# A fused encoder layer on one core: where writes are queued, how weights are cut, and who searches for used tiles

## Chip, cores and metric

One core of one Trainium2 chip runs the kernel as a single program. The metric is the device time of one execution in microseconds, the median of several runs. Each run of the profiler shows one execution.

## The reference

One layer on 256 tokens of width 2048, in fp32. First a residual block: RMSNorm, a projection, trailing mean pools on one half of the columns and eight-head latent attention with a block-causal mask on the other, and an output projection. Then the part around which this change turns, a retrieval over 128 x 128 single-neuron experts:

```python
q = (xn @ w_pq).reshape(B, S, PEER_HEADS, 2, PEER_HALF)
s1 = einsum('bshd,hnd->bshn', q[..., 0, :], sub_k1)
s2 = einsum('bshd,hnd->bshn', q[..., 1, :], sub_k2)
v1, i1 = top_k(s1, 16); v2, i2 = top_k(s2, 16)
vs, ci = top_k((v1[..., :, None] + v2[..., None, :]).reshape(B, S, 8, 256), 16)
eidx = e1 * 128 + e2            # per token: 8 heads x 16 experts
gates = softmax(vs)
act = gelu(einsum('tkd,td->tk', expert_u[eidx], xn))
y = einsum('tk,tkd->td', act * gates, expert_v[eidx])
```

Last, a gate on the layer's own input p: `h + sigmoid(RMSNorm(h) @ w_ple_gate) * (p @ w_ple_proj)`.

## The kernel before, in words

**Products.** TensorE (PE) computes every large product in fp32 accuracy from three passes over split operands: `hi` is the value rounded to fp32r (ScalarE, ACT, L101) and `lo` the rest (VectorE, DVE, L103; now and then GpSimd, POOL). Weights come as units of 128 x 2048 fp32 (1 MB), each used in two parts of 1024 columns. The class `Feed` (L61 to L112) does the loading, two units ahead of the one in use, into three buffers `raw`, all on the queue of SyncE (SP) except the very first unit; it splits two parts ahead into three buffers each of `hi` and `lo`. `mm3` (L213) issues the three matmuls.

**Experts.** The kernel computes the hidden value of all tokens for 112 of the 128 expert tiles densely (the loop at L1441, `feat_mm`, 48 matmuls of 256 columns a tile), and for the last 16 tiles (`NP`, `P0` = 104) only for the pairs that were chosen. Beside the dense tiles run two lists of tasks: `side` (one task per `hook`, two to four hooks a tile) and `lq` for the chosen pairs (0.65 of a task per hook, `PAIR_PACE`).

- *One-hot groups* (`group_hots` L986, `group` L1001): for each of 64 groups of four tokens DVE compares indices with column numbers (two operations at L993) and multiplies by two bf16 parts of the gate (two at L996), ACT makes the third part (L227); 12 bf16 matmuls (L1006) turn them into the gates of all 128 tiles, which DVE multiplies into the activations (L1012) and ACT copies elsewhere (L1014, L1017). Every second group the gates of the 16 pair tiles are written to the tensor `gateD` (L1019).
- *Pairs* (`pair_loads` L1079, `pair_step` L1094): 9 chunks of 128 rows, 8 steps each. POOL gathers a half row of xn per row (`xr`, one buffer) for every four steps and a half row of U (`ur`, two buffers) for every step, two steps ahead; DVE takes the dot product (L1097). After a chunk POOL scatters its four columns of sums to `hidD` (L1104). At the end four quarters are read back, passed through gelu, multiplied by the gates and written to the coefficient tensor `coefD` (L1107 to L1136).
- *Used search and lists*: when the groups are through (about tile 67), `used` (L1189) looks in blocks of eight tiles for pairs of expert and token block with any coefficient; `classes` to `indices` (L1218 to L1337) build lists of the rows of V that are needed, in three stages (tiles 0 to 79, 80 to 119, 120 to 127).
- *Values*: 97 list tiles of V (`v_tile` L1407); POOL gathers rows of V (L1363) and coefficients (L1376). Eleven of them run between the last dense tiles. Half of the V rows use the `raw` buffers of `Feed`.

**Order.** SP's queue keeps the order in which the program emits it; the other engines are ordered by the framework's scheduler, except in two stretches written by hand. Every DMA waits on its issuing queue until its data and its buffer are ready, and what is queued behind it on that engine waits as well. The writes to `coefD` of the dense tiles (L1170) stay on SP's queue in both versions.

Of the kernel before, what the change touches and what calls it, by code (L numbers as in the profile page):

```python
# [8 lines left out]
F32 = mybir.dt.float32  # L9
# [10 lines left out]
P = 128  # L20
# [40 lines left out]
class Feed:  # L61


    def __init__(self, nc, pool, units, loads=2, splits=2, on_pool=()):
        self.nc, self.pool, self.units = nc, pool, units
        self.loads, self.splits, self.on_pool = loads, splits, on_pool
        self.raw = {}
        self.parts = [(u, i) for u, (_, cols, parts, _) in enumerate(units) for i in range(parts)]
        self.ready = deque()
        self.n_load = self.n_split = self.n_got = 0  # L70
        self.end = len(units)

    def load(self, upto):
        while self.n_load < min(upto + 1, self.end):
            src, cols, parts, by_part = self.units[self.n_load]
            if callable(src):
                self.raw[self.n_load] = src()
                self.n_load += 1
                continue
            raw = self.pool.tile([P, 2048], F32, name="raw", tag="raw")  # L80
            w = cols // parts
            if by_part:
                for i in range(parts):
                    self.nc.scalar.dma_start(raw[:, i * w:(i + 1) * w], src[:, i * w:(i + 1) * w])
            else:
                self.nc.sync.dma_start(raw[:, :cols], src)
            self.raw[self.n_load] = raw
            self.n_load += 1

    def split(self, upto):  # L90
        while self.n_split < min(upto + 1, len(self.parts)):
            u, i = self.parts[self.n_split]
            if u >= self.end:
                break
            self.load(u)
            _, cols, parts, _ = self.units[u]
            w = cols // parts
            r = self.raw[u][:, i * w:(i + 1) * w]
# [8 lines left out]
    def get(self):  # L107
        u, _ = self.parts[self.n_got]
        self.load(u + self.loads)
# [5 lines left out]
def emit(tc, a):  # L115
# [82 lines left out]
    feed_v = Feed(nc, strm, [(lambda c=c, i=i: vst["load"](c, i), D, 2, False) for c, i in order[BETWEEN:]], loads=3,  # L198
# [99 lines left out]
    feed.load(0)  # L298
# [377 lines left out]
    e1T = gt.tile([P, T, 2], BF16, name="e1T")  # L676
    e2T = gt.tile([P, T, 2], BF16, name="e2T")
    gT = gt.tile([P, 2, T, 2], BF16, name="gT")
# [4 lines left out]
    iotab = gt.tile([P, P], BF16, name="iotab")  # L683
# [3 lines left out]
    iota1 = gt.tile([P, P], BF16, name="iota1")  # L687
    for lo, hi, base in ((0, P0, 0), (P0, ND, STAGES[2]), (ND, NE, P0)):
        pool.iota(iota1[:, lo:hi], pattern=[[1, hi - lo]], base=base, channel_multiplier=0,
# [149 lines left out]
    def pair_chunks():  # L839
# [5 lines left out]
        for t in range(2):  # L845
            sp.dma_start(listD[t * P * NCH:(t + 1) * P * NCH, :].rearrange("(p k) c -> p (k c)", k=NCH), kd[:, t, :])
# [61 lines left out]
    def slots_T(t):  # L908
# [4 lines left out]
        dve.tensor_copy(e1T[:, ts, :], pt[:, 0:P, None].to_broadcast([P, P, 2]))  # L913
        dve.tensor_copy(e2T[:, ts, :], pt[:, P:2 * P, None].to_broadcast([P, P, 2]))
# [4 lines left out]
        for i in range(3):  # L919
            dve.tensor_copy(part, rest)  # L920
            if i < 2:
                dve.tensor_copy(gT[:, i, ts, :], part[:, :, None].to_broadcast([P, P, 2]))
# [63 lines left out]
    def group_hots(g):  # L986
        wk = st["wk"]
        sh = [P, 4, 64, 2]
        tk = slice(4 * g, 4 * g + 4)
# [11 lines left out]
    def group(g):  # L1001
# [16 lines left out]
        if g % 2 == 1:  # L1018
            sp.dma_start(gateD[:, g // 2].rearrange("p n t -> p (n t)"), st["gs"].rearrange("p n t -> p (n t)"))  # L1019
# [5 lines left out]
    lst = {"n": 0, "x": {}, "u": {}}  # L1025
    steps = [(s, half, i) for s in range(NS) for half in range(2) for i in range(4)]

    def pairs_index():
        lp = st["lp"]
        zt = lp.tile([P, ring_w], F32, name="xr", tag="xr")[:, :1024]  # L1030
        pool.memset(zt, 0.0)
        for i in range(0, NP * T, 1024):
            sp.dma_start(hid_pairs[:, i:i + 1024], zt[:, :min(1024, NP * T - i)])
# [9 lines left out]
    def pairs_index2():  # L1043
        lp, keys = st["lp"], lst["keys"]
        n = 4 * NS
        scr = lp.tile([P, ring_w], F32, name="xr", tag="xr")
# [32 lines left out]
    def pair_loads(k):  # L1079
# [4 lines left out]
        if i == 0:  # L1084
            x = lp.tile([P, ring_w], F32, name="xr", tag="xr")[:, :1024]
# [8 lines left out]
    def pair_step(k):  # L1094
# [5 lines left out]
        if half == 1 and i == 3:  # L1100
            hp = lst["hp"][:, :, s]
            dve.tensor_tensor(hp[:, 0], hp[:, 0], hp[:, 1], op=OP.add)
            for c in range(4):
                pool.indirect_dma_start(out=hidD, out_offset=bass.IndirectOffsetOnAxis(  # L1104
                    ap=lst["hidx"][:, s, c:c + 1], axis=0), in_=hp[:, 0, c:c + 1], in_offset=None)

    def pair_load_coefs(q):  # L1107
        lp = st["lp"]
# [3 lines left out]
        sp.dma_start(hq, hid_pairs[:, q * w:(q + 1) * w])  # L1112
        sp.dma_start(gq, gateD.rearrange("p a n t -> p (a n t)")[:, q * w:(q + 1) * w])
        lst["hg"] = hq, gq

    def pair_coefs(q):
# [4 lines left out]
        cq = lp.tile([P, ring_w], F32, name="xr", tag="xr")[:, :NP * 64].rearrange("p (n t) -> p n t", t=64)  # L1121
# [6 lines left out]
        sp.dma_start(coef_rows[1][:, P0 - N0:P0 - N0 + NP, 64 * q:64 * q + 64], cq)  # L1128
# [60 lines left out]
    def used(lo, hi, b):  # L1189
# [3 lines left out]
        tc.keep_in_program_order(dve.tensor_reduce(  # L1193
# [614 lines left out]
```

## Time and profile before

| | |
|---|---|
| median of 3 runs | 1670.56 us (1669.11 to 1674.48) |
| the profiled execution | 1667.58 us, of which the span from first to last instruction is 1665.8 us |
| mean granted clock of TensorE | 0.978 |
| busy: PE, DVE, ACT, POOL | 1580.7, 1253.8, 884.8, 448.6 us |
| moved by DMA | 396.20 MB, mean 238 GB/s |

The span falls into stages: the attention block up to about 230 us, the search for experts to 383, the dense expert tiles to about 1215 (those with groups and most pair steps from 552 to 898), the values to about 1560, the gate to the end. A busy engine says little here: what a stage costs is read from the idle time of PE, from who ended it, and from the granted clock.

### The profile page before, as it was taken

The page shows a single profiled execution, that of the slowest core. Times are in us where ns is not written, and L with a number is a line of the kernel's source. Part 1 is how long each engine was busy: PE and PEld are TensorE (multiplying, and loading weights), DVE is VectorE, ACT ScalarE, POOL GpSimd, SP SyncE. Part 2 cuts the span into 40 slices and gives each one's busy share as a digit, 9 for nine tenths or more (in the row PEclk, how much of TensorE's full clock was granted, in tenths as well). Part 3 has the DMA queues.
Part 4 walks back from the last instruction along what each step waited for, and adds up shares of the span by engine and source line. Part 5 has one row for each costly group of instructions (what it writes and reads, how often), then busy time and mean ns, then how long its engine had stood idle before and what let it go on. Part 6 is the DMA issues. An engine that isn't in the chain of part 4 may idle for free.

```text
span 1665.8 us, 27633 instructions
## 1 busy us (share of the span) xinstructions
PE 1580.7 (95%) x10548; PEld 1426.5 (86%) x10548; DVE 1253.8 (75%) x2360; ACT 884.8 (53%) x1615; POOL 448.6 (27%) x372
## 2 busy tenths in 40 slices
PE   8999999999999998978888989999989999999998
PEld 6888788999999997867788989999868888888886
DVE  6575667999997887867788868867787667667764
ACT  7765445544544665645454333445455565566653
POOL 0010000000000334533334320032247676676000
PEclk9999999999999999979989999999999999999999
DMA  8652356555555686857668987878679888888462
GB/s 302 222 199 102 127 214 241 178 171 184 178 181 182 214 272 235 261 194 257 231 227 317 351 326 240 291 293 284 206 269 338 288 294 298 282 298 288 152 225 105
DMA packets 82160, 396.20 MB, mean 238 GB/s; under 512 B 19523, under 2 KB 24772, under 8 KB 43620
## 3 DMA queue, kind: packets, MB, share of 16 engines
q1 hardware_dynamic: 48148, 233.87, 39.6%
q0 software_dynamic: 32000, 157.48, 27.5%
q10 hardware_dynamic: 1872, 3.02, 0.5%
q8 instruction: 84, 1.38, 0.3%
q14 instruction: 56, 0.46, 0.1%
HBM read 367.01 MB, written 27.32 MB: 237 GB/s over the span
## 4 chain that ended last, share of the span: by engine, by line
PE 72%; DMA 12%; DVE 8%; issue 3%; ACT 3%; POOL 1%; SPq 0%; DVEq 0%; ACTq 0%; POOLq 0%
PE bank L216 23%; PE bank L215 23%; PE bank L214 23%; DMA raw<-in_U 5%; DMA ur<-in_UP,uidx 3%; DVE lo L103 3%; DVE ur L1097 2%; ACT hi L101 2%; DMA xr<-xnD,rowx 2%; DMA raw<-in_w_in_q 1%; DVE oo L996 1%; PE bank L1310 1%; DVE oo L993 1%; PE bank L1006 1%; DMA raw<-in_w_out 1%
## 5 line engine op out<-in xcount | busy, mean ns | idle before, releaser
L101 ACT CAST hi<-raw 128x1024 fp32r<-128x1024 f32 (+2 forms) x466 | 479.0, 1032 | 460.2 <-PE bank L215 261.8
L103 DVE TENSOR_TENSOR lo<-raw,hi 128x1024 fp32r<-128x1024 f32 (+2 forms) x466 | 558.0, 1201 | 197.2 <-ACT hi L101 195.8
L214 PE MATMUL bank<-xnH,hi 128*128 128x256 f32 x1792 | 522.2, 292 | 6.0 <-ACT hi L101 6.0
L216 PE MATMUL bank<-xnH,lo 128*128 128x256 f32 x1792 | 518.2, 290 | 6.6 <-DVE lo L103 6.4
L215 PE MATMUL bank<-xnL,hi 128*128 128x256 f32 x1792 | 516.2, 288 | 0.0
L214 PEld LDWEIGHTS bank<-xnH,hi 128*128 128x128 f32 x1792 | 351.2, 196 | 8.5 <-ACT hi L101 6.9
L216 PEld LDWEIGHTS bank<-xnH,lo 128*128 128x128 f32 x1792 | 350.3, 196 | 9.5 <-DVE lo L103 8.8
L215 PEld LDWEIGHTS bank<-xnL,hi 128*128 128x128 f32 x1792 | 351.2, 196 | 0.3
L215 PE MATMUL bank<-lo,ccH 128*128 128x512 f32 x520 | 206.3, 397 | 1.1 <-DVE lo L103 1.1
L216 PE MATMUL bank<-hi,ccL 128*128 128x512 f32 x520 | 205.7, 396 | 0.0
L103 DVE TENSOR_TENSOR lo<-vraw,hi 128x1024 fp32r<-128x1024 f32 x108 | 131.4, 1224 | 51.0 <-ACT hi L101 49.7
L1376 POOL DMA_INDIRECT cr<-coefD,idx x97 | 127.5, 1315 | 144.4 <-DVE idx L1337 73.0
L214 PE MATMUL bank<-hi,ccH 128*128 128x512 f32 x520 | 154.5, 395 | 1.1 <-ACT hi L101 1.1
L101 ACT CAST hi<-vraw 128x1024 fp32r<-128x1024 f32 x110 | 115.1, 1049 | 64.6 <-PE bank L216 41.6
L1090 POOL DMA_INDIRECT ur<-in_UP,uidx x72 | 85.2, 1184 | 168.9 <-DVE hp L1097 134.3
L1097 DVE CUSTOM_DVE_ANT_0 ur<-ur,xr 128x1024 f32<-128x1024 f32 x72 | 87.6, 1220 | 56.7 <-DMA xr<-xnD,rowx 28.6
L215 PEld LDWEIGHTS bank<-lo,ccH 128*128 128x128 f32 x520 | 98.3, 189 | 24.7 <-DVE lo L103 2.3
L214 PEld LDWEIGHTS bank<-hi,ccH 128*128 128x128 f32 x520 | 97.5, 189 | 24.0 <-ACT hi L101 2.0
L216 PEld LDWEIGHTS bank<-hi,ccL 128*128 128x128 f32 x520 | 98.3, 189 | 22.3
L1006 PE MATMUL bank<-oo 128*128 128x128 bf16 x768 | 75.7, 228 | 39.7 <-DVE oo L996 37.5
L227 ACT ACTIVATE oo<-oo,gT 128x128 bf16<-128x128 bf16 x256 | 82.4, 399 | 46.7 <-DVE oo L996 45.9
L1006 PEld LDWEIGHTS <-oo 128*128 128x128 bf16 x768 | 49.1, 101 | 50.9 <-DVE oo L996 37.1
(398 smaller groups left out, 2474.6 us busy)
## 6 DMA issues: line engine op xcount, KB each, us to landing
raw<-in_U SPq DMA_DIRECT2D x112, 1024.0 KB, 5.6
raw<-in_w_out SPq DMA_DIRECT2D x16, 1024.0 KB, 4.9
raw<-in_w_pq SPq DMA_DIRECT2D x16, 1024.0 KB, 4.9
raw<-in_w_gate SPq DMA_DIRECT2D x16, 1024.0 KB, 5.0
raw<-in_w_in_p SPq DMA_DIRECT2D x8, 1024.0 KB, 4.8
coefD<-CA SPq DMA_DIRECT2D x8, 1024.0 KB, 12.0
coefD<-CB SPq DMA_DIRECT2D x5, 1024.0 KB, 10.6
raw<-in_w_in_kv SPq DMA_DIRECT2D x8, 576.0 KB, 4.6
```

Source lines behind the costliest of these rows:

```text
L101: self.nc.scalar.copy(hi[:, :w], r)
L103: eng.tensor_tensor(lo[:, :w], r, hi[:, :w].bitcast(F32), op=OP.subtract)
L214: pe.matmul(ps, ah, bh, start=start, stop=False)
L215: pe.matmul(ps, ah, bl, start=False, stop=False)
L216: pe.matmul(ps, al, bh, start=False, stop=stop)
L227: act.activation(dst, ps, AF.Copy, scale=scale)
L993: dve.tensor_tensor(pairs(dst), cols.rearrange("p (i c) -> p i c", c=2)[:, None].to_broadcast(sh), e[:, tk, None, :].to_broadcast(sh), op= ...
L996: dve.tensor_tensor(pairs(oo[:, k]), pairs(m1), gT[:, k, tk, None, :].to_broadcast(sh), op=OP.mult)
L1006: pe.matmul(pt[:, i * P:(i + 1) * P], o2, o1[k], start=(k == 0), stop=(k == 2))
L1090: pool.indirect_dma_start(out=u, out_offset=None, in_=a["UP"], in_offset=bass.IndirectOffsetOnAxis(ap=lst["uidx"][:, half, s, i:i + 1], ax ...
L1097: dve.tensor_tensor_reduce(out=u, in0=u, in1=lst["x"][s, half], scale=1.0, scalar=0.0, op0=OP.mult, op1=OP.add, accum_out=lst["hp"][:, hal ...
L1376: pool.indirect_dma_start(out=cr[:, :w], out_offset=None, in_=src, in_offset=bass.IndirectOffsetOnAxis(ap=row(c, i, 1), axis=0))
```

## The change

Seven edits in one diff, all of them shown in their core:

- `Feed` loads parts (half units) instead of units: five buffers of 1024 columns instead of three of 2048, five parts ahead.
- V rows that used the `raw` buffers get three buffers `vraw2` of their own, in the space of the last stage.
- Writes (and the reads of the pair quarters) move from SP's queue: `gateD` to ACT's, `xnD`, `listD`, the zeros of `hidD`, the pair quarters and their coefficients to POOL's; the last are written in two halves.
- `xr` gets two buffers.
- The scatters to `hidD` are queued and issued one at a time at odd steps; what is left goes before the quarters are read.
- The two index tables and the two gate tables each become one, so that two wide operations make the one-hots of a group.
- `used` becomes eight ACTIVATEs with accumulation on ACT, except for the last stage.

```diff
 class Feed:
...
+    def __init__(self, nc, pool, units, loads=5, splits=2, on_pool=()):
...
     def load(self, upto):
-        while self.n_load < min(upto + 1, self.end):
-            src, cols, parts, by_part = self.units[self.n_load]
+
+        while self.n_load < min(upto + 1, len(self.parts)):
+            u, i = self.parts[self.n_load]
+            if u >= self.end:
+                break
+            src, cols, parts, by_part = self.units[u]
+            w = cols // parts
+            cs = slice(i * w, (i + 1) * w)
             if callable(src):
...
-            raw = self.pool.tile([P, 2048], F32, name="raw", tag="raw")
...
+                raw = self.pool.tile([P, 1024], F32, name="raw", tag="raw", bufs=5)[:, :w]
+                (self.nc.scalar if by_part else self.nc.sync).dma_start(raw, src[:, cs])
             self.raw[self.n_load] = raw
             self.n_load += 1
...
     def get(self):
-        u, _ = self.parts[self.n_got]
-        self.load(u + self.loads)
+        self.load(self.n_got + self.loads)
         self.split(self.n_got + self.splits)
...
-        sp.dma_start(xnD[t * P:(t + 1) * P, :], h[t])
+        pool.dma_start(xnD[t * P:(t + 1) * P, :], h[t])
...
     def group_hots(g):
...
-        for dst, cols, e in ((m1, iota1, e1T), (oo[:, 3], iotab, e2T)):
-            dve.tensor_tensor(pairs(dst), cols.rearrange("p (i c) -> p i c", c=2)[:, None].to_broadcast(sh),
-                              e[:, tk, None, :].to_broadcast(sh), op=OP.is_equal)
-        for k in range(2):
-            dve.tensor_tensor(pairs(oo[:, k]), pairs(m1), gT[:, k, tk, None, :].to_broadcast(sh), op=OP.mult)
+        sh = [P, 2, 4, 64, 2]
+
+        def pairs2(x):
+            return x.rearrange("p a t (i c) -> p a t i c", c=2)
+
+        dve.tensor_tensor(pairs2(oo[:, 2:4]), iotas.rearrange("p a (i c) -> p a i c", c=2)[:, :, None].to_broadcast(sh),
+                          eT[:, g][:, :, :, None, :].to_broadcast(sh), op=OP.is_equal)
+        dve.tensor_tensor(pairs2(oo[:, 0:2]), pairs(m1)[:, None].to_broadcast(sh),
+                          gT[:, g][:, :, :, None, :].to_broadcast(sh), op=OP.mult)
...
-            sp.dma_start(gateD[:, g // 2].rearrange("p n t -> p (n t)"), st["gs"].rearrange("p n t -> p (n t)"))
+            act.dma_start(gateD[:, g // 2].rearrange("p n t -> p (n t)"), st["gs"].rearrange("p n t -> p (n t)"))
...
-            x = lp.tile([P, ring_w], F32, name="xr", tag="xr")[:, :1024]
+            x = lp.tile([P, ring_w], F32, name="xr", tag="xr", bufs=2)[:, :1024]
...
-            for c in range(4):
-                pool.indirect_dma_start(out=hidD, out_offset=bass.IndirectOffsetOnAxis(
-                    ap=lst["hidx"][:, s, c:c + 1], axis=0), in_=hp[:, 0, c:c + 1], in_offset=None)
+            lst["out"].extend((s, c) for c in range(4))
+        elif lst["out"] and (k % 2 or k == len(steps) - 1):
+            pair_out()
+
+    def pair_out():
+        s, c = lst["out"].popleft()
+        pool.indirect_dma_start(out=hidD, out_offset=bass.IndirectOffsetOnAxis(
+            ap=lst["hidx"][:, s, c:c + 1], axis=0), in_=lst["hp"][:, 0, s, c:c + 1], in_offset=None)
 
     def pair_load_coefs(q):
+        while lst["out"]:
+            pair_out()
...
-        sp.dma_start(hq, hid_pairs[:, q * w:(q + 1) * w])
-        sp.dma_start(gq, gateD.rearrange("p a n t -> p (a n t)")[:, q * w:(q + 1) * w])
+        pool.dma_start(hq, hid_pairs[:, q * w:(q + 1) * w])
+        pool.dma_start(gq, gateD.rearrange("p a n t -> p (a n t)")[:, q * w:(q + 1) * w])
...
-        sp.dma_start(coef_rows[1][:, P0 - N0:P0 - N0 + NP, 64 * q:64 * q + 64], cq)
+        for lo in range(0, NP, 8):
+            hi = min(lo + 8, NP)
+            pool.dma_start(coef_rows[1][:, P0 - N0 + lo:P0 - N0 + hi, 64 * q:64 * q + 64], cq[:, lo:hi])
...
-        tc.keep_in_program_order(dve.tensor_reduce(
-            st["used"][:, b, lo:hi], C[:, lo - o:hi - o, b * P:(b + 1) * P], axis=AX.X, op=OP.max,
-            apply_absolute_value=True))
+        if lo >= STAGES[2]:
+            tc.keep_in_program_order(dve.tensor_reduce(
+                st["used"][:, b, lo:hi], C[:, lo - o:hi - o, b * P:(b + 1) * P], axis=AX.X, op=OP.max,
+                apply_absolute_value=True))
+            return
+        for i in range(lo, hi):
+            jk = st["wk"].tile([P, P], BF16, name="jk", tag="jk")
+            act.activation(jk, C[:, i - o, b * P:(b + 1) * P], AF.Abs, accum_out=st["used"][:, b, i:i + 1])
...
-            raw = strm.tile([P, D], F32, name="raw", tag="raw")
+            raw = pl.tile([P, D], F32, name="vraw2", tag="vraw2", bufs=3)
```

## Rows read from the trace of the kernel before

**Rows 1.** Busy time of each engine by stage; columns as in the first line.

```profile
core 0: us, PE busy (x) PEld busy (x) DVE busy (x) ACT busy (x) POOL busy (x), PEclk, DMA share, GB/s
...
310.00:552.00 242.00, 242.00 (x2039) 241.83 (x2039) 221.32 (x613) 109.46 (x140) 3.37 (x4) 1.00 0.52 179
552.00:898.00 346.00, 297.81 (x2594) 283.54 (x2593) 270.94 (x572) 197.00 (x593) 138.61 (x119) 0.92 0.71 239
898.00:946.00 48.00, 46.95 (x382) 46.14 (x383) 45.44 (x52) 18.96 (x24) 11.43 (x8) 1.00 0.98 381
...
988.00:1108.00 120.00, 113.46 (x953) 112.08 (x952) 94.38 (x186) 47.45 (x61) 16.54 (x14) 0.99 0.79 274
...
1250.00:1666.00 416.00, 408.07 (x1782) 331.87 (x1780) 276.41 (x319) 239.03 (x314) 203.72 (x151) 0.99 0.73 256
```

**Rows 2.** Timeline of ACT, 1100:1112: start us, us, instruction (one gelu ends a tile).

```profile
1103.38 0.38 ACT L1153 ACTIVATE gl<-bank 128x256 f32<-128x256 f32 x1
...
1109.14 0.38 ACT L1153 ACTIVATE gl<-bank 128x256 f32<-128x256 f32 x1
```

**Rows 3.** Groups of instructions of DVE in 552:898: count, busy us, mean ns, idle before.

```profile
L103 DVE TENSOR_TENSOR lo<-raw,hi 128x1024 fp32r<-128x1024 f32 x75 | 91.1, 1218 | 19.7 <-ACT hi L101 19.7
L1097 DVE CUSTOM_DVE_ANT_0 ur<-ur,xr 128x1024 f32<-128x1024 f32 x60 | 72.9, 1219 | 47.2 <-DMA xr<-xnD,rowx 28.6 <-DMA ur<-in_UP,uidx 18.5
L996 DVE TENSOR_TENSOR oo<-oo,gT 128x512 bf16<-128x512 bf16 x126 | 47.8, 420 | 0.0
```

**Rows 4.** The same of PE in 552:898.

```profile
L1006 PE MATMUL bank<-oo 128*128 128x128 bf16 x768 | 75.7, 228 | 39.7 <-DVE oo L996 37.5 <-ACT oo L227 1.8
```

**Rows 5.** Timeline of PE, 700.6:701.0.

```profile
700.42 0.72 PE L1006 MATMUL bank<-oo 128*128 128x128 bf16 x10
```

**Rows 6.** Waits of DVE in 552:898: us in total, times, longest us.

```profile
DVE ur L1097 <- DMA xr<-xnD,rowx: 28.6, 9, 6.6
DVE lo L103 <- ACT hi L101: 19.7, 20, 4.5
DVE ur L1097 <- DMA ur<-in_UP,uidx: 18.5, 10, 6.6
```

**Rows 7.** Waits of ACT in 552:898.

```profile
ACT hi L101 <- DMA raw<-in_U: 41.4, 22, 6.4
```

**Rows 8.** Waits of SP's queue in 552:898.

```profile
SPq L1019 <- ACT gs L1017: 175.5, 18, 16.6
```

**Rows 9.** Waits of POOL in 552:898.

```profile
POOL hidD L1104 <- DMA hidD<-hp,hidx: 49.5, 16, 7.7
```

**Rows 10.** Timeline of SP's queue, 700:710: one issue of a gate write.

```profile
707.20 0.34 SPq L1019 DMA_DIRECT2D gateD<-gs  x1
```

**Rows 11.** DMA issues of the whole run: count, KB each, median us to landing.

```profile
raw<-in_w_proj SPq DMA_DIRECT2D x4, 512.0 KB, 4.3
...
ur<-in_UP,uidx POOLq DMA_INDIRECT x72, 5.6
```

**Rows 12.** Timeline of DVE, 704:709.

```profile
704.01 0.41 DVE L993 TENSOR_TENSOR oo<-iota,e1T 128x512 bf16<-128x512 bf16 x1
704.34 0.42 DVE L993 TENSOR_TENSOR oo<-iotab,e2T 128x512 bf16<-128x512 bf16 x1
```

**Rows 13.** Groups by shape, whole run: a bf16 operation on 392 elements.

```profile
L1298 DVE TENSOR_TENSOR oh<-iotab,lf 128x392 bf16<-128x392 bf16 x32 | 11.4, 358 | 6.1 <-PE bank L1310 6.1
```

**Rows 14.** Groups of DVE in 898:946.

```profile
L1193 DVE TENSOR_REDUCE used<-CA 128x8 f32<-128x1024 f32 x15 | 18.2, 1213 | 0.0
```

**Rows 15.** Timeline of ACT, 99.4:101.2.

```profile
99.80 0.30 ACT L509 ACTIVATE junk<-kv 128x128 f32<-128x128 f32 x1
...
100.67 0.30 ACT L509 ACTIVATE junk<-kv 128x128 f32<-128x128 f32 x1
```

**Rows 16.** Timeline of POOL, 995:1014: the last four scatters.

```profile
997.04 1.19 POOL L1104 DMA_INDIRECT hidD<-hp,hidx  x1 [13.02 <-DVE hp L1102]
...
1012.28 0.97 POOL L1104 DMA_INDIRECT hidD<-hp,hidx  x1 [2.37 <-DMA hidD<-hp,hidx]
```

More of the change, by code (lines that the diff above doesn't have):

```diff
@@ L61, with start @@
 class Feed:
-    def __init__(self, nc, pool, units, loads=2, splits=2, on_pool=()):
-        self.nc, self.pool, self.units = nc, pool, units
+    def __init__(self, nc, pool, units, loads=5, splits=2, on_pool=()):
+        self.nc, self.pool = nc, pool
         self.loads, self.splits, self.on_pool = loads, splits, on_pool
-        self.raw = {}
+        self.start(units)
+    def start(self, units):
+        self.units = units
         self.parts = [(u, i) for u, (_, cols, parts, _) in enumerate(units) for i in range(parts)]
+        self.raw, self.tiles = {}, {}
         self.ready = deque()
@@ L73, in load, with load_units @@
     def load(self, upto):
[L74 to L86 removed]
+        while self.n_load < min(upto + 1, len(self.parts)):
[5 more added lines that the diff above has]
+            cs = slice(i * w, (i + 1) * w)
+            if callable(src):
+                if i == 0:
+                    self.tiles[u] = src()
+                raw = self.tiles[u][:, cs]
+            else:
+                raw = self.pool.tile([P, 1024], F32, name="raw", tag="raw", bufs=5)[:, :w]
+                (self.nc.scalar if by_part else self.nc.sync).dma_start(raw, src[:, cs])
             self.raw[self.n_load] = raw
             self.n_load += 1
+    def load_units(self, upto):
+        self.load(max(n for n, (u, _) in enumerate(self.parts) if u <= upto))
     def split(self, upto):
         while self.n_split < min(upto + 1, len(self.parts)):
[L92 to L93 removed]
+            if self.parts[self.n_split][0] >= self.end:
                 break
[L95 to L98, printed above, removed]
+            self.load(self.n_split)
+            r = self.raw.pop(self.n_split)
+            w = r.shape[-1]
             hi = self.pool.tile([P, 1024], F32R, name="hi", tag="hi")
@@ L197, in emit @@
     feed.end = held
-    feed_v = Feed(nc, strm, [(lambda c=c, i=i: vst["load"](c, i), D, 2, False) for c, i in order[BETWEEN:]], loads=3,
+    feed_v = Feed(nc, strm, [(lambda c=c, i=i: vst["load"](c, i), D, 2, False) for c, i in order[BETWEEN:]], loads=7,
                   on_pool=ON_POOL)
@@ L296, in split_x @@
             split_scaled(xH[:, kt, :], xL[:, kt, :], src, g_mix[:, kt:kt + 1])
-    feed.load(0)
+    feed.load_units(0)
     xr = load_x(0)
@@ L1502, in emit @@
     flush()
-    feed.load(held - 1)
+    feed.load_units(held - 1)
     while spans:
@@ L1576, in emit @@
             feed.end = len(units)
-            feed.load(held + 1)
+            feed.load_units(held + 1)
     def tail(acc, pl, h2, last, filler):
@@ L1724, in emit @@
                 again.append((a["w_gate"][n, g], 2048, 2, False))
-        feed.units, feed.parts = again, [(u, i) for u in range(16) for i in range(2)]
-        feed.n_load = feed.n_split = feed.n_got = 0
-        feed.raw = {}
-        feed.end = len(again)
+        feed.start(again)
         tail(acc, fb, h2, lambda add_values: [add_values(n) for n in range(2)], lambda: None)
```

35 lines of the change are left out of this document (17 added, 18 removed).

## The prediction

> **The bound now.** I read the stages first, then for the worst stage the waits of each engine, then durations and intervals of the instructions the change touches. In most stages TensorE (PE) is full: 242.00 of 242.00 us in 310:552, 408.07 of 416.00 in 1250:1666 [rows 1]. The exception is 552:898, where the pair list and the one-hot groups run beside the expert tiles: PE is busy 297.81 of 346.00 us and its granted clock averages 0.92, so part of that time ran at the lower of its two levels (1.2 instead of 2.4 GHz). In 310:552, where PE is never idle, the mean is 1.00.
>
> How much of the 346 us is needed? An undisturbed expert tile takes 5.76 us [rows 2] and is two halves of 2.88. The stage splits 75 halves [rows 3]: 216 us. It also has 768 group matmuls [rows 4]; ten take 0.72 us, the last of them 0.228, so one starts every 0.055 us [rows 4, 5]: 42 us. PE needs 258 us, 88 fewer than it gets: 48 idle, 28 of slow clock (0.08 of 346), the rest small. VectorE (DVE) is busy 270.94 us [rows 1], also near a bound, and in order; it has three long waits [rows 6]: x rows 28.6 us, the hi half from ScalarE (ACT) 19.7, rows of U 18.5. What PE waits for is DVE, late by these.
>
> Each has a visible cause. ACT's hi waits 41.4 us for raw weights [rows 7], while the SP queue sits at L1019 for the gate values of ACT (175.5 us in 18 waits is the longest of four such entries) [rows 8] with the next weight load queued behind. The x rows have one buffer, so their load can't be issued before the last step on the old ones. The U rows have two, but POOL, which issues them, stands 49.5 us on the four scatters of a chunk, each waiting for the one before to land [rows 9].
>
> **The change, part by part.** The sum is against the profiled execution, 1667.6 us (span 1665.8 and 1.8 around it), 3.0 below the median 1670.6; 3.0 is added at the end.
>
> Gate writes on ACT's queue: SP loses its long waits and weights are requested when a buffer is free. The lead hardly changes: three tiles of two halves before, five halves now, 14 us at 2.88 each. DVE's 19.7 falls to about 4, what ACT's own waits for PE leave (bounds 0 and 19.7). The 32 issues stand on ACT instead, before the next hi or evacuation; ACT is busy 197.00 of 346 [rows 1], so they cost nothing; without that cover, 32 times 0.34 us [rows 10], 11 us.
>
> Two x buffers: the load goes out ahead of the wait for U's buffer, a step earlier; 28.6 goes to 0 (bounds 0 and 10). Next to be late is U.
>
> Scatters spread, one at every second step: POOL's 49.5 us goes. U rows keep two buffers, so their round remains: a step of 1.22 [rows 3], 5.6 from issue to landing [rows 11], and the issue itself, some 8 us for two steps, 240 for 60. That fits, but the same bytes in a shorter stage land later. I take 15 for the 18.5 (bounds 5 and 40).
>
> One-hots in two operations: 126 multiplications [rows 3] and about as many comparisons of 512 elements become some 125 operations of 1024. No row shows 1024 bf16 elements with two inputs. A 512 starts 0.33 us after its neighbour [rows 12]; 420 ns at 512 [rows 3] and 358 at 392 [rows 13] give 0.52 ns an element, so 0.60 between starts at 1024, against 0.67 for two. The upper bound is the 1.22 us of the fp32 operation on 1024 [rows 3], were the packed rate lost; the lower is 0.60. I take 0.60, since type and the innermost pair stay as they are: 125 times 0.07, 9 us less. DVE's work: 262.
>
> So the stage: 262 of DVE, with waits of 4 (hi), 15 (U), 8 for PE (more than now, as DVE runs closer behind it) and 5 of small ones: 294 instead of 346. **Minus 52.** PE's 258 lies below. The slow clock goes with the idle time and is inside this difference.
>
> Used search on ACT: 26 DVE reductions of 1.21 us (15 of them stand in 898:946 [rows 14]) become 208 pairs of ACTIVATE and accumulator read. The nearest rows, square sums over 128 columns, start 0.29 us apart (0.87 for three) [rows 15], so eight take 2.3 us. PE lacked little there (46.95 busy of 48.00 [rows 1]), so little is gained. ACT gets 18 calls within nine tiles: 42 us on top of 18.96 busy, 61 in 48. Its halves run two ahead of PE, 5.8 us less 2.2 for the split itself, so some 4 of the 13 over are swallowed, and 2 more since busy times overlap. **Plus 7** (bounds minus 1, PE's idle time, and plus 13). The other 8 calls come two in eight tiles and hide behind PE.
>
> Coefficient loads and writes on POOL: SP in 988:1108 no longer stands on them. PE idles 6.5 us there [rows 1], part of it for late weights: **minus 2** (0 to minus 6). On POOL they wait for DVE's products with the gathers of coefficients for the values queued behind; POOL is busy 16.54 of 120 us, so that is taken as covered.
>
> End of the scatters: the code releases one at every odd step but not at a chunk's last, three for every four queued; with nine chunks 12 remain, drained at once before the coefficients are read, where 4 were. Four start within 15.2 us [rows 16], 5.1 apart, so 8 more take 41. The next two task slots and the lead hide part, and these tiles are needed tens of us later; the danger is an ACT or DVE instruction that waits for them in order with hi behind it. No row shows such a wait. **Plus 6** (0 to 41).
>
> At nothing: the start (five halves requested ahead instead of two tiles; fewer bytes compete with the first parts; minus 2 to plus 4); xnD, list and zero writes on POOL, 8 in all, beside a POOL busy at most 138.61 of 346 us; V rows in buffers that come free when the coefficients of the last tiles have landed (the third load needs them first; without that lead the 416 us stage would start some us later); and halves of 512 KB: a load of that size lands in 4.3 us [rows 11] and five in flight cover it. If not, see the last rival.
>
> Sum: 1667.6 - 52 + 7 - 2 + 6 = 1626.6; with 3.0 to the median, **1630**.
>
> The Trainium skill ("DMA: Bandwidth & Descriptors", Issuing engines are not separate DMA queues) says that all issuers share the same DMA engines and that several issuers save only the sequencer's issue time, usually small. The trace differs: SP's time at L1019 is waiting in order, 0.34 us of it issuing. By the rule alone the move would bring nothing, the second rival's result.
>
> **The rivals.** (1) The waits move: with x and weights on time, U rows bind. The round of 8 us for two steps grows to 10.3 with denser traffic (239 GB/s now) and POOL's other issues between: 30 rounds are 309, with 9 for uneven hooks 318. For it: two buffers only. Against: 5.6 was taken with the scatters in the way. Minus 28: 1654.
>
> (2) The queue move is worth nothing: SP still blocks on coefficient writes, or freed buffers are the limit, and 19.7 stays. 262 + 19.7 + 15 + 8 + 5 = 310, minus 36: 1646. Against: nearly all of SP's wait there is L1019.
>
> (3) Better: the waits all but vanish and the stage takes 270: minus 76, 1606.
>
> (4) Slower: the wide one-hots lose the packed rate. 125 operations at 1.22 instead of 0.67 make DVE's 271 into 340; with waits of 32 the stage takes 372, plus 26: 1667.6 + 26 + 7 - 2 + 6 + 3 = 1708. DVE's other work is 187, so from 0.93 us an operation (187 + 116 + 32 = 335, minus 11) the gain only pays the other terms. For it: one more dimension in the pattern. Against: the innermost pair is unchanged.
>
> (5) Slower too: halves don't overlap. Two loads of 4.3 one behind the other are 8.6 for a tile of 5.76, 2.84 over on some 42 tiles in 310:552 (242 / 5.76): plus 119, 1749. The 381 GB/s of 898:946 with mixed sizes speak against it.
>
> **Chances.** Forecast 0.54, (1) 0.22, (2) 0.06, (3) 0.08, (4) 0.08, (5) 0.02. (1) to (3) are faster too; within the forecast the drain of scatters and ACT at their bounds (41 and 13) would together bring 1671, so I move 0.04 to no change. A measurement here tells 0.3%, 5 us. Faster 0.86, same 0.04, slower 0.10. The range leaves out (4), (5) and the far ends of the unknown costs: 1605 to 1658.
>
> **What would show it.** Right: x waits on DVE gone; SP's waits in the stage for buffers alone; 552:898 shrunk to 285 to 305 with PE's clock near 1.00; one-hots of about 0.68 us; ACT nearly full for nine tiles after the groups; 12 scatters in a row after the last pair step. Wrong: a one-hot above 0.9 us; DVE waiting for U as long as for x and U before; ACT or DVE idle on the coefficient loads; PE idle in 310:552 behind raw.

## The result: slower, and the profile after

The change makes the kernel slower: 1715.5 us (median of 4 runs, 1709.95 to 1723.89) against 1670.95 for the kernel before, ratio 1.0268 [1.0223, 1.0314] (in brackets the 95% interval, here and below). The profiled span grew from 1665.8 to 1713.1 us. TensorE's expert tiles mark off the program: a tile begins with the first `xnH`, `lo` matmul of its 48. By these marks the 47 us arise here (us):

| stretch | before | after | ordered (below) |
|---|---|---|---|
| start to tile 0 | 383.2 | 388.6 | 386.9 |
| tiles 0 to 29 | 169.0 | 169.1 | 169.1 |
| tiles 29 to 67, the group stage | 345.9 | 381.7 | 286.8 |
| tiles 67 to 82 | 90.1 | 104.3 | 99.9 |
| tiles 82 to 100 | 120.1 | 113.0 | 131.3 |
| the rest | 557.4 | 556.5 | 560.0 |

Almost everything turns on the group stage: plus 35.8 where I had forecast minus 52. Its busy times after the change, with the two stages behind it (columns as in the first line; they answer to [rows 1]):

```profile
core 0: us, PE busy (x) PEld busy (x) DVE busy (x) ACT busy (x) POOL busy (x), PEclk, DMA share, GB/s
...
557.00:939.00 382.00, 303.98 (x2598) 290.57 (x2596) 276.41 (x468) 201.54 (x614) 175.59 (x141) 0.90 0.72 239
939.00:1044.00 105.00, 92.91 (x724) 90.27 (x725) 55.09 (x65) 94.63 (x356) 10.38 (x14) 0.96 0.82 281
1044.00:1157.00 113.00, 113.00 (x954) 112.03 (x953) 77.17 (x164) 54.21 (x123) 13.37 (x10) 0.99 0.66 234
```

VectorE has little more to do than before (276.41 against 270.94 us, with twelve more pair steps), TensorE idles 78 us instead of 48, and its granted clock falls from 0.92 to 0.90. The waits of VectorE in 557:939 (us in total, times, longest) say what for; they answer to [rows 6]:

```profile
DVE ur L1106 <- DMA ur<-in_UP,uidx: 77.1, 44, 5.6
DVE xr L1143 <- DMA ur<-gateD: 13.4, 1, 13.4
DVE lo L110 <- ACT hi L108: 4.1, 4, 1.8
```

The wait for x is gone, that for hi has fallen from 19.7 to 4.1, both as forecast. But the wait for rows of U has grown from 18.5 to 77.1 us. One more view shows why, the groups of VectorE in 557:939 (count | busy us, mean ns | idle before), which answer to [rows 3]:

```profile
L1106 DVE CUSTOM_DVE_ANT_0 ur<-ur,xr 128x1024 f32<-128x1024 f32 x72 | 88.2, 1225 | 80.2 <-DMA ur<-in_UP,uidx 77.1 <-issue 2.0 <-DVE lo L110 0.9
L1004 DVE TENSOR_TENSOR oo<-oo,gT 128x1024 bf16<-128x1024 bf16 x63 | 43.3, 688 | 0.2
L1002 DVE TENSOR_TENSOR oo<-iotas,eT 128x1024 bf16<-128x1024 bf16 x62 | 42.3, 683 | 0.8 <-PE bank L1015 0.8
```

All 72 pair steps now stand within the stage, where 60 stood before. No line of the diff moves a step: held in the order that the program gives, the steps lie over 110 halves of weights in the kernel before and 116 in the changed one (`bkeep` and `keep` below). The framework's scheduler orders VectorE's instructions, and it has packed them: between the first and the last step VectorE splits 98 halves before and 62 after. A U buffer's round can't follow. The timeline of VectorE shows one wait and what stands behind it in order (start us, us, instruction [idle before]):

```profile
761.56 1.22 DVE L110 TENSOR_TENSOR lo<-raw,hi 128x1024 fp32r<-128x1024 f32 x1
762.70 0.68 DVE L1004 TENSOR_TENSOR oo<-oo,gT 128x1024 bf16<-128x1024 bf16 x1
765.96 1.23 DVE L1106 CUSTOM_DVE_ANT_0 ur<-ur,xr 128x1024 f32<-128x1024 f32 x1 [2.57 <-DMA ur<-in_UP,uidx]
...
767.38 0.68 DVE L1002 TENSOR_TENSOR oo<-iotas,eT 128x1024 bf16<-128x1024 bf16 x1
767.98 1.22 DVE L110 TENSOR_TENSOR lo<-raw,hi 128x1024 fp32r<-128x1024 f32 x1
```

The step waits 2.57 us for U, and the next one-hots and the next lo, which TensorE needs, wait behind it. TensorE's waits in 557:939 end at the same place:

```profile
PE bank L1015 <- DVE oo L1004: 67.2, 25, 6.5
PE bank L220 <- ACT hi L108: 8.5, 1, 8.5
```

The first of the 72 steps starts at 576.6 and the last at 903.6: 4.6 us apart, 9.2 for two, where I had reckoned 8 for two. The second line of TensorE's waits belongs to the end of the list: behind the last step ScalarE, like VectorE (13.4, above), waits for the coefficients of the pairs, with hi behind it:

```profile
ACT ur L1138 <- DMA ur<-hidD: 13.4, 1, 13.4
```

VectorE didn't wait there in the kernel before.

### The profile page after: what moved, and what is told of

Read it like the earlier page. It is cut to its first block, busy times and chain, and to the rows that moved or that the text cites. A ratio compares the mean times of both kernels' runs of the same rounds, so it can differ in the third digit from the quotient of the medians.

```text
span 1713.1 us, 28379 instructions
## 1 busy us (share of the span) xinstructions
PE 1593.5 (93%) x10548; PEld 1440.4 (84%) x10548; DVE 1219.0 (71%) x2206; ACT 959.0 (56%) x2031; POOL 475.7 (28%) x396
## 4 chain that ended last, share of the span: by engine, by line
PE 54%; DMA 10%; issue 8%; DVE 4%; ACT 4%; POOL 3%; POOLq 0%; DVEq 0%; ACTq 0%
PE bank L220 17%; PE bank L221 17%; PE bank L222 17%; DMA ur<-in_UP,uidx 7%; ACT jk L1218 2%; DMA hidD<-hp,hidx 2%; POOL ur L1099 2%; ACT hi L108 1%; DVE lo L110 1%; DMA ur<-gateD 1%; PE bank L1333 1%; POOL hidD L1118 1%; DMA ur<-hidD 1%; DVE ur L1106 1%; POOL keys L1048 1%
## 5 line engine op out<-in xcount | busy, mean ns | idle before, releaser
L108 ACT CAST hi<-raw 128x1024 fp32r<-128x1024 f32 (+2 forms) x382 | 391.9, 1027 | 377.3 <-PE bank L221 249.2
L110 DVE TENSOR_TENSOR lo<-raw,hi 128x1024 fp32r<-128x1024 f32 (+2 forms) x382 | 456.6, 1197 | 193.2 <-ACT hi L108 190.7
L220 PE MATMUL bank<-xnH,hi 128*128 128x256 f32 x1792 | 528.1, 295 | 11.0 <-ACT hi L108 11.0
L220 PEld LDWEIGHTS bank<-xnH,hi 128*128 128x128 f32 x1792 | 356.2, 199 | 13.1 <-ACT hi L108 12.3
L222 PEld LDWEIGHTS bank<-xnH,lo 128*128 128x128 f32 x1792 | 354.6, 198 | 8.9 <-DVE lo L110 8.3
L221 PEld LDWEIGHTS bank<-xnL,hi 128*128 128x128 f32 x1792 | 355.5, 198 | 0.5
L110 DVE TENSOR_TENSOR lo<-vraw,hi 128x1024 fp32r<-128x1024 f32 x192 | 233.7, 1225 | 86.8 <-ACT hi L108 86.6
L108 ACT CAST hi<-vraw 128x1024 fp32r<-128x1024 f32 x194 | 203.2, 1049 | 93.1 <-PE bank L222 72.6
L1386 POOL DMA_INDIRECT vraw<-in_V,idx x97 | 130.5, 1345 | 125.9 <-DVE lo L110 54.9
L1106 DVE CUSTOM_DVE_ANT_0 ur<-ur,xr 128x1024 f32<-128x1024 f32 x72 | 88.2, 1225 | 80.2 <-DMA ur<-in_UP,uidx 77.1
L1099 POOL DMA_INDIRECT ur<-in_UP,uidx x72 | 95.3, 1323 | 111.4 <-DVE hp L1106 73.6
```

The lines of the kernel that those rows point to most:

```text
L108: self.nc.scalar.copy(hi[:, :w], r)
L110: eng.tensor_tensor(lo[:, :w], r, hi[:, :w].bitcast(F32), op=OP.subtract)
L220: pe.matmul(ps, ah, bh, start=start, stop=False)
L221: pe.matmul(ps, ah, bl, start=False, stop=False)
L222: pe.matmul(ps, al, bh, start=False, stop=stop)
L1099: pool.indirect_dma_start(out=u, out_offset=None, in_=a["UP"], in_offset=bass.IndirectOffsetOnAxis(ap=lst["uidx"][:, half, s, i:i + 1], ax ...
```

## The experiments

Theory A: the parts of the change do what they should, but the scheduler's new order puts the steps closer than two U buffers come round. Theory B: the order is innocent. Times are medians; the kernel before gave 1670 to 1673 beside them.

**1. The order alone, and three buffers** (`keep`, `ur3r4`).

```diff
-        dve.tensor_tensor_reduce(out=u, in0=u, ...)
+        tc.keep_in_program_order(dve.tensor_tensor_reduce(out=u, in0=u, ...))
```

> The changed kernel with one more line: the multiply-and-sum of every pair step is kept in the order in which the program gives it, so the 72 steps lie over 116 halves of VectorE's order instead of 62. Nothing is left out. Theory A (the scheduler packed the steps into the group stage, one per 5.3 us, faster than two U buffers come round): about 48 of the 72 steps are left in tiles 29 to 67; a step every 6 us is slower than the round of U, so VectorE's 77 us of waits for U fall below 20 and the stage goes from 381.7 to 290-310 us; the kernel takes 1630-1660 us. Theory B (the order is innocent; the wide one-hots, the gate writes on ScalarE or denser traffic make the stage long): the waits for U may move, but the stage stays within 15 us of 382 and the kernel within 1700-1725.

Measured: 1638.38 us, 0.9787 [0.9754, 0.9819] of the kernel before and 77 us below the changed kernel. The group stage takes 286.8 us with 47 steps in it (116 halves from first to last). Its row and VectorE's waits in 557:843:

```profile
557.00:843.00 286.00, 274.55 (x2586) 265.74 (x2585) 243.88 (x412) 199.86 (x616) 114.16 (x92) 0.99 0.77 254
```

```profile
DVE ur L1106 <- DMA ur<-in_UP,uidx: 29.7, 9, 6.7
DVE lo L110 <- ACT hi L108: 5.1, 7, 1.3
```

TensorE idles 11 us and the clock is back at 0.99. Theory A holds; the waits for U stay above the 20 I expected. This version beats both kernels.

```diff
-        u = lp.tile([P, ring_w], F32, name="ur", tag="ur", bufs=2)[:, :1024]
+        u = lp.tile([P, ring_w], F32, name="ur", tag="ur", bufs=3)[:, :1024]
...
-    def __init__(self, nc, pool, units, loads=5, splits=2, on_pool=()):
+    def __init__(self, nc, pool, units, loads=4, splits=2, on_pool=()):
...
-                raw = self.pool.tile([P, 1024], F32, name="raw", tag="raw", bufs=5)[:, :w]
+                raw = self.pool.tile([P, 1024], F32, name="raw", tag="raw", bufs=4)[:, :w]
```

> The changed kernel with three buffers for the rows of U in place of two, paid for with four weight buffers of half a tile in place of five (four halves asked for ahead). Nothing is left out. The scheduler now packs the 72 steps into 51 halves. Theory A (the round of a U buffer, about 6.2 us landing + 1.3 issue + 1.2 step, sets the pace): a step can come every 2.9 us instead of 4.4 or more; the steps take about 210 us, the waits for U fall from 77 to 15-35 us although the order is tighter, the stage to 290-320, the kernel to 1635-1665. Theory B (contention: more loads in flight land later in proportion): landing grows from 6.2 to 9 us, the waits stay at 60-90, the kernel at 1700-1725. If four weight buffers are too few, waits of VectorE or ScalarE on raw tell it.

Measured: 1691.13 us, between the two expectations. In the trace (of the slowest run, 1702 us) the stage takes 365.6 us, above theory A's 290 to 320, and the waits for U in 562:841 are 45.5 us, though the steps now come every 3.65 us (582.0 to 841.1, 71 intervals). The groups of GpSimd in that stretch:

```profile
L1099 POOL DMA_INDIRECT ur<-in_UP,uidx x72 | 93.4, 1297 | 57.5 <-DVE hp L1106 26.5 <-DVE CA L1021 11.2 <-issue 8.2
L1118 POOL DMA_INDIRECT hidD<-hp,hidx x32 | 44.0, 1376 | 44.0 <-DMA hidD<-hp,hidx 26.6 <-issue 17.0 <-DVE oo L1002 0.3
```

A third buffer speeds the round but doesn't end the wait. GpSimd issues gathers and scatters in order and stands 44.0 us ahead of scatters, with the gathers behind them; how much of the rest is this and how much the transfers themselves stays open.

**2. How close the steps stand** (`kp075`, `kp085`). From `keep`, at other paces:

```diff
-PAIR_PACE = 0.65
+PAIR_PACE = 0.75    (kp085: 0.85)
```

> The changed kernel with pair steps kept in order, at a pace of 0.75 a hook instead of 0.65: 106 halves, some 56 steps within tiles 29 to 67 instead of 46. Nothing is left out. If what sets the price is how close the steps stand against the round of two U buffers (5.3 us a step), 56 steps need 297 us: that stretch goes from 287 to 295-310 while 67 to 100 lose 8 to 15; in all 1632-1645. Rival (a step costs its 1.22 us wherever it stands): 287 + 12 and the same taken off later, 1638 plus or minus 3.

> The same at a pace of 0.85: 92 halves, some 62 steps within tiles 29 to 67. Nothing is left out. By the round of U 62 steps need 329 us there: 320-340, VectorE waiting 45-65 us for U; 67 to 100 lose 20; in all 1645-1670. Rival (1.22 us a step): 287 + 20 and 20 off later, 1635-1642.

Measured: 1652.10 and 1658.18. With the other kernels (halves and steps counted in the traces, stage times by the tile marks, waits from the waits of VectorE in the stage):

| kernel | halves | steps in the stage | stage, us | wait for U, us | median, us |
|---|---|---|---|---|---|
| `keep` | 116 | 47 | 286.8 | 29.7 | 1638.4 |
| `kp075` | 106 | 54 | 303.9 | 34.8 | 1652.1 |
| `kp085` | 93 | 60 | 325.7 | 44.1 | 1658.2 |
| after | 62 | 72 | 381.7 | 77.1 | 1715.5 |

Seven more steps cost 17.1 us, the next six 21.8 and the next twelve 56.0: 2.4, 3.6 and 4.7 us a step, not the 1.22 of VectorE's work. The closer the steps stand, the more the wait for U adds, as theory A has it. From `keep` to the changed kernel that wait grows by 47.4 us and the steps' own work by 30.5, together 78 of 94.9; the rest isn't traced, and the changed kernel, whose steps aren't held in order, differs in more than the pace. Both stage times lie within the expectation, `kp085`'s wait just under it; later tiles give back less than I expected of `kp075` (2.5 us instead of 8 to 15), so its total lies 7 above the range.

**3. What made the scheduler pack the steps** (`b_gact`). The kernel before with one line of the change:

```diff
-            sp.dma_start(gateD[:, g // 2]...)
+            act.dma_start(gateD[:, g // 2]...)
```

> The kernel before with one edit: the gate values are written on ScalarE's queue. Nothing is left out. The scheduler then puts the 72 pair steps over 79 halves instead of 98. By my prediction's term this edit alone gains 16 us (hi no longer late), 1650-1660. Theory A (taking a wait away makes the scheduler pack the steps, and the rows of x and U can't follow): it gains nothing or loses, 1670-1710, with VectorE's waits for x and U above 70 us in tiles 29 to 67 (28.6 and 18.5 before) and its wait for hi below 10.

Measured: 1702.41 us, 1.0210 [1.0176, 1.0245] of the kernel before. The steps lie over 79 halves instead of 98; 67 of the 72 steps stand in the stage, which takes 384.0 us. VectorE's waits in 552:936:

```profile
DVE ur L1097 <- DMA xr<-xnD,rowx: 50.9, 15, 6.5
DVE ur L1097 <- DMA ur<-in_UP,uidx: 49.1, 19, 7.5
...
DVE lo L103 <- ACT hi L101: 0.3, 1, 0.3
```

The wait for hi is gone (19.7 to 0.3), yet the kernel is 32 us slower: the wait for x has gone from 28.6 to 50.9, that for U from 18.5 to 49.1. So the queue move by itself changes the order and costs more than it gains. Which other parts took it from 79 to 62 halves wasn't run.

**4. The order without the change** (`bkeep`). The same line as in `keep`, in the kernel before.

> The kernel before with one edit: its pair steps are kept in program order too (72 steps over 110 halves of VectorE's order instead of 98). Nothing is left out. Theory A (the order is what the change lost by, its parts are what it wins by): the kernel before gains little from it, since x rows, the blocked SyncE queue and the scatters stay as they are: 1655-1675. Rival (the order alone makes the 77 us between the changed kernel and its ordered form, the parts are worth little): 1630-1650.

Measured: 1688.15 us, slower than before (1.0117 [1.0086, 1.0147]) and outside both expectations. The stage falls to 310.4 us with 47 steps, but tiles 82 to 100 grow from 120.1 to 180.3. The waits of SyncE's queue in 949:1129:

```profile
SPq L1113 <- DMA hidD<-hp,hidx: 82.4, 1, 82.4
SPq L86 <- DVE lo L103: 34.3, 7, 7.4
SPq L1129 <- DVE xr L1128: 26.8, 4, 7.9
```

Late steps make late scatters; the read of the coefficients waits for them at the head of SyncE's queue for 82.4 us, with all weights behind it. In this kernel the order loses more behind the stage than it gains there. The queue of the coefficients is only part of that: `kcoefsp` (below) has them on SyncE too, beside the other parts of the change, and there the same wait is 41.3 us and the kernel loses 9. The parts need the order, and the order needs the parts; which of them it needs most wasn't run.

**5. One part undone at a time**, each from `keep`. First, gate writes on SyncE again (`kgsp`) and one x buffer (`kxr1`, `bufs=2` taken off the four `xr` tiles of the pairs):

```diff
-            act.dma_start(gateD[:, g // 2]...)
+            sp.dma_start(gateD[:, g // 2]...)
```

> The changed kernel with the pair steps kept in program order, and one part of the change undone: the gate values are written on SyncE's queue again. Nothing is left out. My sum of the prediction gives the queue move 16 us (ScalarE's late hi, 19.7 down to 4). If that holds: SyncE stands some 150 us at the gate writes, ScalarE waits 30-40 us for raw weights, tiles 29 to 67 grow from 286.8 to 297-307, the kernel from 1638 to 1648-1660. Rival (five halves asked for ahead hide the blocked queue, so the move is worth nothing): within 4 us of 1638.

> The same base (pair steps kept in order) with one buffer for the rows of x, as before the change. Nothing is left out. My sum gives the second buffer 28.6 us of waits. If that holds: VectorE waits 15-30 us more, for x at every fourth step, tiles 29 to 67 take 298-315 and the kernel 1648-1665. Rival (with steps 6 us apart the x rows hide, or their wait only takes the place of that for U): within 5 us of 1638.

Measured: `kgsp` 1667.59 (0.9967 [0.9944, 0.9989]), 29 us more than `keep`; `kxr1` 1680.30 (1.0045 [1.0022, 1.0067]), 42 more. Both parts are worth more than my terms of 16 and 28.6. (The traced runs of `kgsp` and `keep`, 1676.5 and 1635.6, lie further apart than the medians.) In `kgsp`, 557:876, SyncE's queue (first row) and ScalarE (second) wait again as before the change [rows 7, 8], and the stage takes 320.8 us:

```profile
SPq L1028 <- ACT gs L1026: 193.3, 22, 16.1
```

```profile
ACT hi L108 <- DMA raw<-in_U: 26.0, 14, 7.7
```

The Trainium skill ("DMA: Bandwidth & Descriptors", Issuing engines are not separate DMA queues) says that DMAs from several engines at once save only the time that it takes to initiate them. By that rule alone the move would be worth nothing; the 193.3 us are waiting in order, and the measurement decides against it here. Not all of the 29 us is late hi, as the term had it: VectorE's wait for hi in 557:876 is 15.8 us against 5.1 in `keep`, that for U 45.2 against 29.7; why U is later, no run shows. In `kxr1`, 556:873, the wait for x stands beside that for U:

```profile
DVE ur L1106 <- DMA ur<-in_UP,uidx: 31.5, 10, 7.0
DVE ur L1106 <- DMA xr<-xnD,rowx: 21.7, 7, 4.7
```

Its stage takes 318.1 us, 31.3 more than `keep`'s.

Next, four narrow one-hot operations (`knarrow`) and the four scatters at a chunk's end (`kscat4`):

```diff
-        dve.tensor_tensor(pairs2(oo[:, 2:4]), iotas..., eT[:, g]..., op=OP.is_equal)
-        dve.tensor_tensor(pairs2(oo[:, 0:2]), pairs(m1)..., gT[:, g]..., op=OP.mult)
+        for a2 in range(2):
+            dve.tensor_tensor(pairs(oo[:, 2 + a2]), iotas[:, a2]..., eT[:, g, a2]..., op=OP.is_equal)
+        for a2 in range(2):
+            dve.tensor_tensor(pairs(oo[:, a2]), pairs(m1), gT[:, g, a2]..., op=OP.mult)
```

> The same base with the one-hots of a group in four operations of 512 elements again. Nothing is left out. VectorE's work in tiles 29 to 67 grows from 244 to 251-253 us of 287. If VectorE bounds the stage, the kernel takes 5-10 us more than 1638; if TensorE (275 us busy there) does, within 3 us of 1638.

```diff
-        elif lst["out"] and (k % 2 or k == len(steps) - 1):
-            pair_out()
+            while lst["out"]:
+                pair_out()
```

> The changed kernel with pair steps kept in order, and the four scatters of a chunk issued together at its end again, so none is left to drain after the last step. Nothing is left out. By the prediction's terms GpSimd stands 10-20 us more on scatters in tiles 29 to 67 and the waits for U grow there by 5-15 us, while the drain (plus 6, bounds 0 and 41) goes: 1636-1648. Rival (spreading is worth nothing, since GpSimd stands on each scatter anyway, 39.2 us in the base, and the drain makes VectorE wait 19.0 us for the coefficients): tiles 67 to 100 gain 5-15 us, 1625-1634.

Measured: `knarrow` 1646.76, 8.4 more than `keep`, as the expectation has it for a stage bound by VectorE (253.70 us busy in 557:858; the stage takes 301.7, 14.9 more, of which 6 come back behind it). `kscat4` 1638.52, no difference: GpSimd stands on scatters 40.4 us in 557:845, against 39.2 in `keep` (557:843), and VectorE's wait for the coefficients in 843:1080 is 20.0 against 19.0. But the edit tests nothing: in the traces of `keep` and `kscat4` the gathers and scatters of the pairs stand on GpSimd in the same order, for the scheduler orders GpSimd too. It had spread the scatters in the kernel before as well, where the code issues four together (GpSimd's timeline, 610:640):

```profile
615.29 1.09 POOL L1104 DMA_INDIRECT hidD<-hp,hidx  x1 [0.30 <-DVE CA L1012]
620.83 0.96 POOL L1090 DMA_INDIRECT ur<-in_UP,uidx  x1 [4.45 <-DVE hp L1097]
622.10 1.20 POOL L1104 DMA_INDIRECT hidD<-hp,hidx  x1 [0.30 <-issue]
623.84 1.12 POOL L1090 DMA_INDIRECT ur<-in_UP,uidx  x1 [0.54 <-DVE CA L1012]
626.14 1.75 POOL L1104 DMA_INDIRECT hidD<-hp,hidx  x1 [1.18 <-DMA hidD<-hp,hidx]
```

What spreading is worth, no run shows.

Then the coefficients on SyncE (`kcoefsp`) and more buffers at the start (`kstart`):

```diff
-        pool.dma_start(hq, hid_pairs[...])
-        pool.dma_start(gq, gateD...)
+        sp.dma_start(hq, hid_pairs[...])
+        sp.dma_start(gq, gateD...)
...
-        for lo in range(0, NP, 8):
...
-            pool.dma_start(coef_rows[1][...], cq[:, lo:hi])
+        sp.dma_start(coef_rows[1][...], cq)
```

> The same base with the reads of the pair coefficients and their write on SyncE's queue again (the write in one piece). Nothing is left out. The prediction gave this move 2 us (0 to 6); the changed kernel gained 7 in tiles 82 to 100. So plus 2 to plus 8: 1640-1647. Rival (SyncE blocks but five halves ahead cover it): within 2 us of 1638.

Measured: 1647.55, 9 more than `keep` and just above the expectation; tiles 82 to 100 take 148.9 us instead of 131.3. SyncE's queue in 943:1092:

```profile
SPq L1129 <- DMA hidD<-hp,hidx: 41.3, 1, 41.3
SPq L1145 <- DVE xr L1144: 23.9, 3, 10.2
```

```diff
...
+                if self.early is not None and self.n_load < 40 and self.n_load % 7 > 4:
+                    raw = self.early.tile([P, 1024], F32, name="raw0", tag="raw0", bufs=2)[:, :w]
...
-        self.load(self.n_got + self.loads)
+        self.load(self.n_got + (7 if self.early is not None and self.n_got < 31 else self.loads))
```

> The same base with two more half buffers for the first 40 weight halves alone (a buffer of the front stage's memory; seven asked for ahead of use instead of five while they last). Nothing is left out. Theory A (the 4 to 5 us lost before tile 0 come from less weight memory, 20 KB a partition instead of 24, so fewer bytes in flight: 262 GB/s instead of 324 in the first 30 us): tile 0 starts at 381-384 instead of 386.9, the kernel takes 1632-1636. Rival (they come from the halves themselves, smaller loads and twice the issues on SyncE): tile 0 within 1.5 us of 386.9.

Measured: tile 0 starts at 382.5 us, as before the change (383.2). The rows of 0:30, first of the changed kernel, then of `kstart`:

```profile
0.00:30.00 30.00, 23.95 (x96) 18.86 (x97) 17.29 (x27) 18.32 (x31) 2.30 (x19) 1.00 0.76 262
```

```profile
0.00:30.00 30.00, 24.02 (x98) 18.99 (x99) 17.94 (x29) 18.06 (x31) 1.55 (x13) 1.00 0.80 285
```

So the loss at the start is weight memory, with the requests ahead that it allows: five halves hold 20 KB a partition, three whole buffers 24, the seven of `kstart` 28. Yet the total is 1640.10, above the 1632 to 1636 expected: the 4.4 us are gone again in the group stage (293.2) and tiles 82 to 100 (142.6). Why, with steps that end 7 us later, stays open.

**6. The used search** (`useddve`, from the changed kernel; `both`, from `keep`).

```diff
-        for i in range(lo, hi):
...
-            act.activation(jk, C[:, i - o, ...], AF.Abs, accum_out=st["used"][:, b, i:i + 1])
+        dve.tensor_reduce(st["used"][:, b, lo:hi], C[:, lo - o:hi - o, ...], op=OP.max, ...)
```

> The changed kernel with the used search back in VectorE reductions, in all groups. Nothing is left out. Theory A (the 14 us lost in tiles 67 to 82 are ScalarE's, full with the search: hi comes late): that stretch falls from 104.3 to 90-95 us, the kernel to 1701-1706. Theory B (the stretch is long because VectorE and ScalarE wait there for the drained scatters and the coefficients): it stays above 100, the kernel within 1710-1720.

> The two edits together: pair steps kept in program order, used search on VectorE. Nothing is left out. Theory A: the gains add, 1620-1650, 8 to 14 us less than with the order alone. If VectorE, which then carries 24 late steps and the search in the same tiles, becomes the bound there, the search is worth nothing or costs up to 10 us: 1640-1670.

Measured: `useddve` 1706.54, 9 less than the changed kernel; tiles 67 to 82 take 92.9 us instead of 104.3. There the search on ScalarE is a loss. `both` 1643.49, 5 more than `keep`: there, by the totals, it is a gain. In `keep`, VectorE carries late steps in those tiles and `both` gives it the search too (82.96 us busy in 844:940, against 61.98 in 843:943); tiles 67 to 82 gain 4.1 us, but behind tile 100 `both` takes 567.9 against 560.0, 7 of it in tiles 100 to 111, which I can't explain; so that the search itself makes the difference isn't shown.

**7. Three U buffers in order** (`k3`): `keep` with the edits of `ur3r4`.

> The same base with three buffers for the rows of U in place of two and four weight buffers of half a tile in place of five. Nothing is left out. In the base VectorE still waits 30.4 us for U in 10 waits in 557 to 843. Theory A (two buffers are the cause of what is left): these fall below 10, the stage from 286.8 to 268-280, the kernel to 1618-1632. Rival (the waits come from GpSimd, which issues gathers and scatters in order and stands on the scatters): they stay above 20, the kernel within 5 us of 1638. If four weight buffers are too few, the start loses 5 us more, as it did with the scheduler's order (tile 0 at 393.5 instead of 388.6).

Measured: 1643.52, 5 more than `keep` and outside theory A's 1618 to 1632. VectorE's wait for U in 557:841 falls from 29.7 to

```profile
DVE ur L1106 <- DMA ur<-in_UP,uidx: 9.6, 3, 4.9
```

and the stage to 279.4: two buffers are the cause of what is left. Four weight buffers take it back: tile 0 starts at 392.9 (386.9), tiles 67 to 82 take 108.9 (99.9).

## Why the prediction was wrong

**The step that failed** is in the group stage's term: "some 8 us for two steps, 240 for 60. That fits". It took from the trace of before that 60 steps stand in the stage. The order of VectorE's instructions isn't in the code but made anew by the scheduler, and the diff gave it other waits. 72 stood there, the wait for U was 77.1 us instead of 15 (bounds 5 and 40), and the stage lost 35.8. The count alone wouldn't have broken the sum: at 8 us for two, 72 steps need 288, inside the 294. At the measured 4.6 each they take 327, over only 62 of the stage's 75 halves, and the other halves come on top. In the terms of the sum, VectorE's work was 276.4 instead of 262 (twelve more steps), hi 4.1 as forecast, U 77.1 instead of 15, the other waits 10.2 instead of 13, and 13.4 went to the coefficients, which the sum didn't have: 381.2 instead of 294. With the order held (`keep`), the stage takes 286.8 against my 294, though with 47 steps.

**A second error, smaller**: at 60 steps (`kp085`) the stage takes 325.7 us and the kernel 1658.2. That is my first rival (318 us, 1654), not the forecast (1630). Two steps took 8 in the sum and 10.3 in the rival; `kp085` took 5.0 us for one (578.1 to 874.0 for 60). All rivals shared the 60. The two slower rivals weren't it: the fourth ends near the measured time, at 1708, but by one-hots of 1.22 us, and they took 0.68, so that is chance; and the halves overlap (tiles 0 to 29 take 169.1 against 169.0).

**Term by term.**
- Gate writes: hi's wait 4.1 after, as forecast; undone in order, 29 us.
- Two x buffers: the wait is gone, as forecast; undone in order, 42 us, more than the 28.6 of the wait.
- One-hots: 0.60 us between starts forecast, 0.60 in the timeline above (767.38 to 767.98); 9 us of VectorE's work forecast, 8.4 of the total by `knarrow`, but 14.9 in its stage: that the two numbers meet is in part luck.
- Scatters: "POOL's 49.5 us goes" was wrong. The scheduler had spread them before the change already (above). A scatter still waits for the one before it, and a gather behind it. GpSimd's waits in 557:939, to be held against [rows 9]:

```profile
POOL hidD L1118 <- DMA hidD<-hp,hidx: 60.6, 22, 5.0
```

- The drain, plus 6: not twelve scatters stood behind the last step but four (907.6 to 924.5 on GpSimd), as before the change; the scheduler had put the others earlier. The danger that the prediction named is there even so: ScalarE waited 13.4 us for the coefficients with hi behind it, and TensorE 8.5. `kscat4` can't tell what the drain is worth.
- Used search, plus 7: 9.0 in the packed order (`useddve`), inside the bounds, but by a wrong price. I took 0.29 us a pair from [rows 15]; the timeline of ScalarE after the change has 0.44:

```profile
954.29 0.31 ACT L1218 ACTIVATE jk<-CA 128x128 bf16<-128x128 f32 x1
954.51 0.19 ACT L1218 ACTIVATION_READ_ACCUMULATOR jk<-CA 128x1 f32 x1
954.73 0.31 ACT L1218 ACTIVATE jk<-CA 128x128 bf16<-128x128 f32 x1
```

- Coefficients on GpSimd, minus 2: tiles 82 to 100 gained 7.1, though the last pair step and its scatters no longer stand there either; 9 in order by `kcoefsp`.
- The start, 0 (minus 2 to plus 4): plus 5.4, outside its bounds, from less weight memory.

## What to carry to other kernels

Where a scheduler sets the order on an engine, a diff that takes waits away also moves work that it doesn't name: count, in the new program, how many instructions of each kind stand in the stage before any term is reckoned. An edit to the order of issue in the code may change nothing either, so compare the orders in the traces before reading a price from it. Work that waits for a slow transfer in an in-order engine is best held at a pace that its buffers can follow. What one part is worth depends on the order it stands in: the same queue move costs 32 us in one and is worth 29 in another.

## What the runs showed of the hardware

The rows of U took longer to land in the changed kernel: a median of 6.2 us from issue over the whole run, against 5.6 before [rows 11]. How close the steps stand isn't what makes it: in `kscat4`, where they start 6.0 us apart instead of 4.6, it was 6.8. The cause stays open. The rows (count, median us to landing), first after, then `kscat4`:

```profile
ur<-in_UP,uidx POOLq DMA_INDIRECT x72, 6.2
```

```profile
ur<-in_UP,uidx POOLq DMA_INDIRECT x72, 6.8
```

And an ACTIVATE with its accumulator read over 128 columns has no single price: 0.29 us between starts at one line [rows 15], 0.44 at another (above). What makes the difference, no run here shows.
